# Attention scores from split factors, rope's shifts on ScalarE, softmax one step behind, and two small changes, in a two-layer decoder trunk

## The chip, the core and the metric

The kernel runs on one core of a Trainium2 chip. The core has engines that run side by side, each in the order of its own queue: TensorE (PE in the profile; its weight loads are PEld), VectorE (DVE), ScalarE (ACT), GpSimd (POOL), and SyncE (SP), which issues the transfers. The metric is the time of one execution in device microseconds.

## What is computed

The input is 256 tokens of width 2048. Layer 0 is a gated short convolution and a squared-ReLU MLP; layer 1 is latent attention and another such MLP. After each of the four sublayers `x = LN(ALPHA * x + f(x))`. All is float32.

```
ckv  = h @ w_dkv                                  # 512 latents and 64 rope channels
c    = rms_norm(ckv[..., :512]);  k_pe = rope(ckv[..., 512:])
kv   = c @ w_ukv                                  # 16 heads: k_nope 128, v 128
q    = rms_norm(x @ w_dq) @ w_uq                  # 16 heads: q_nope 128, q_pe 64 (rope)
s    = (q_nope @ k_nope.T + q_pe @ k_pe.T) * 192 ** -0.5      # causal mask
o    = softmax(s) @ v;  out = o @ w_o
mlp  = square(relu(x @ w1)) @ w2                  # 2048 -> 8192 -> 2048
```

## The kernel before

**Split products.** A value is cut into a part `hi`, stored in the type fp32r (ScalarE writes it by a copy), and the rest `lo` (VectorE subtracts). A product is then three fp32r products, hi by hi, lo by hi and hi by lo, and PE makes each in one record. A few small products are made from plain f32 instead; each of these is two records on PE. Weights come in units of 512 KB into six buffers (`raws`), are split into a ring of eight (`whl`), and are taken in the order of the list `stream` (`take`).

**Order of the work.** Most of the program is written in the order in which it is wanted, and a scheduler at build time places each engine's instructions by that order and by when their inputs should be ready. Inside the MLPs the order is made by the kernel's own planner (`Work.arrange`): it has a list of operations with costs and due times, and simulates when each could run. At the start of the program `WARM` f32 products of ones are made while the first data are on their way; then the first four weight columns are multiplied as rows of x arrive (`ps_g`).

**Norms.** Before a sublayer's result is added, `Norm.prepare` scales a row block of `xres` by ALPHA and subtracts a mean taken from the first block (`mu0p`, one f32 product with a square of ones). For the norm after the first MLP (index 1) these sixteen operations stand in the planner's list. `to_wide` then turns the MLP's result by transposes and adds it.

**Latents.** Nine products of 258 columns (`ps_w`, the first three `ps_g`) give four blocks of the keys' latent, one of rope channels (given twice, in both halves of the rows) and four of the queries' latent. `latent` weights them, splits them into `chl` and `qhl`, and sums their squares. `rms` turns a sum of squares into a factor per token, by products of one column (`rstat`) and a root; `rkp` spreads it over the rows, giving `rk`. The keys' latents are split unscaled; `rk` and `rc` come in when keys and values leave PSUM.

**Attention.** `project(g)` makes keys, queries, values and rope queries of four heads, in twelve pieces, and `attention(g - 1)` for the group before runs between them, also in twelve. A head's `attend` has three pieces: the scores `S` of two query blocks (128 queries against 128 keys, 128 against 256) with the softmax; the transposes of the probabilities (`tp`); the product with the values (`po`). The scores are four plain f32 products. After the last group the output projection begins (`out_first`, `ps_wo`).

**Rope.** VectorE multiplies by the cosines, then multiplies each quarter of 32 rows by the sines while it writes it into the neighbouring quarter, then adds.

In the kernel's printed form, a helper records most operations on the engines, so nearly all rows of the profile have its line, L71, and are told apart by their tiles. The tiles `kqva` are the arrays of keys, queries, values and probabilities; `lat` are the latents; `nu` is a step of the norm.

Of the kernel before, what the change touches and what calls it, by code (L numbers as in the profile page):

```python
# [44 lines left out]
GROUP = 3  # L45
WARM = 6
WO_G = 3
# [6 lines left out]
def trunk(ctx: ExitStack, tc: tile.TileContext, opening, xT, vecs, w_in, w_out, w_kv, w_q, w_uk, w_uv,  # L54
# [321 lines left out]
    class Norm:  # L376
# [3 lines left out]
        def __init__(self, idx, scale):  # L380
            self.idx, self.scale = idx, scale
            self.S = act.tile([P, T], F32, tag="S", name=f"S{idx}")
            self.Q = act.tile([P, T], F32, tag="Q", name=f"Q{idx}")
            self.mu0 = act.tile([P, T], F32, tag="mu0", name=f"mu0{idx}")
            self.ws = None

        def prepare(self, m):
# [383 lines left out]
    def mlp(idx, ln, after, blocks, fast):  # L771
# [111 lines left out]
        for k in todo:  # L883
# [181 lines left out]
        def put(n, t, ps):  # L1065
            vector.tensor_tensor(block(n, t), block(n, t), ps, ALU.add)
# [31 lines left out]
    with tc.tile_pool(name="att", bufs=1) as ap:  # L1098
        lat = array("c", F32R, "lat", 2 * NK, 2 * T)
        chl, qhl = ([lat[:, k, :] for k in range(o, o + NK)] for o in (0, NK))  # L1100
        kpe = ap.tile([P, 2, T], F32, name="kpe")
        nc.gpsimd.memset(kpe, 0.0)
        rc = ap.tile([P, 2], F32, name="rc")
# [5 lines left out]

        def rope(dst, src, rows):  # L1110

            a = tmp.tile([P, T], F32, tag="sq", name="ropea")
            b = tmp.tile([P, T], F32, tag="nu", name="ropeb")
            vector.tensor_tensor(a[rows], src[rows], cos_t[rows], ALU.mult)
            for s in range(rows.start, rows.stop, 32):
                d = s ^ 32
                vector.tensor_tensor(b[d:d + 32], src[s:s + 32], sin_t[s:s + 32], ALU.mult)
            vector.tensor_tensor(dst[rows], a[rows], b[rows], ALU.add)

        def latent(ps, m, dst, gcol, sqs):  # L1120
            f = tmp.tile([P, T], F32, tag="fh", name="lat", bufs=3)
            ln.weighted(ps, f)
            g = vec[:, gcol + m:gcol + m + 1]
            scalar.activation(dst[m][:, :T], f, AF.Copy, scale=g)
            vector.scalar_tensor_tensor(dst[m][:, T:], f, g, dst[m][:, :T].bitcast(F32),
                                           ALU.mult, ALU.subtract)
            if m == 0:
                scalar.activation(sqs, f, AF.Square)
            else:
                sq = tmp.tile([P, T], F32, tag="sq", name="sq")  # L1130
                scalar.activation(sq, f, AF.Square)
                vector.tensor_tensor(sqs, sqs, sq, ALU.add)

        def rms(out, sqs):
# [6 lines left out]
            rsqrt(out, ve)  # L1141

        csq = act.tile([P, T], F32, tag="S", name="csq")
        qsq = act.tile([P, T], F32, tag="Q", name="qsq")
# [39 lines left out]
        oT = [ot[:, k, :] for k in range(H)]  # L1184
        kq, vp = (array(a, F32, f"kqv{a}", NC * W) for a in ("a1", "a2"))
        k2, q2, v2 = ([r[:, o:o + 1024].rearrange("p (j t) -> p j t", j=J) for o in (b, b + 1024)]
                      for r, b, J in ((kq, 0, 4), (kq, 2048, 4), (vp, 0, 2)))
        p2 = [vp[:, o:o + 512].rearrange("p (j t) -> p j t", j=2) for o in (2048, 2560)]
        pr2 = [vp[:, o:o + 3 * P] for o in (3072, 3456)]

        with tc.tile_pool(name="att2", bufs=2) as a2, \
                tc.tile_pool(name="paux", bufs=1, space=PS) as paux:
            def project(g, box):

                k4, q4, p4, v4 = (t[g % 2] for t in (k2, q2, p2, v2))
                box.update(k=k4, q=q4, p=p4, v=v4)
# [12 lines left out]
                if g == 0:  # L1209
                    query_scale()  # L1210
                for _ in range(2):
                    ln.normal(next(todo))
                w = take()
# [6 lines left out]
                w = take(1)  # L1220
                for j in range(2):
                    ps = psum("ps_p")
                    mm(ps, w, 4 * j, qhl, NK)
                    rope(p4[:, j, :], ps[:, :T], slice(0, P))
                    yield

            def attend(h, box):

                j = h % 4
                qn, kn = box["q"][:, j, :], box["k"][:, j, :]  # L1230
                qp, kp = box["p"][:, j // 2, :], kpe[:, h % 2, :]
# [6 lines left out]
                pr = pr2[h % 2]  # L1238
                mx = small.tile([P, 2], F32, tag="mx", name="mx")
# [25 lines left out]
            def attention(g, box):  # L1265
                gens = [attend(4 * g + j, box) for j in range(4)]
                for step in range(6):
                    for j in range(3, -1, -1):
                        if 0 <= step - j < 3:
                            next(gens[j])  # L1270
                            yield

# [165 lines left out]
```

## Time and profile before

| | us |
|---|---|
| median of three runs | 2000.35 (1997.7 to 2000.36) |
| the profiled execution | 2000.64 |
| its span, first to last instruction | 1998.8 |
| PE busy in it | 1981.9 (99%) |
| VectorE busy | 1763.3 (88%) |
| ScalarE busy | 1392.6 (70%) |

The mean granted TensorE clock is 0.998. Three kinds of rows are used below. A stage's row gives the stretch, its length, and the busy us of PE, PEld, DVE, ACT and POOL with their counts, then the granted clock, the share of the DMA engines and GB/s. A row of the chain of work that ended last gives start, length, and what ran; a count stands for pieces that follow each other. A group's row gives engine, operation, output and inputs, shape, count, then busy us and the mean ns of one, then the idle time ahead of it with what ended it. Records of products overlap: one lasts longer than the distance to the next.

### The profile page before, as it was taken

Reading aid. Unit: us, or ns where it says so; the run is one execution under the profiler, and the core shown is the slowest. Engines: PE = TensorE matmul, PEld = TensorE weight load, DVE = VectorE, ACT = ScalarE, POOL = GpSimd, SP = SyncE. Lnnn points to the kernel's source line nnn. Section 1 sums busy time; section 2 is a strip of 40 time slices with the busy share of each in tenths; the row PEclk is TensorE's granted clock in tenths of the full one; section 3 lists DMA queues with packets and bytes.
Section 4 is the critical chain, followed back from the end, with each engine's and each line's share of the span. In section 5 each row is a group of like instructions: output and inputs, shape, how many; then the busy total and the mean of one; then the engine's idle time right before and its main releaser. Section 6 shows DMA issues by size and latency. Waiting matters only on the chain.

```text
span 1998.8 us, 29668 instructions
## 1 busy us (share of the span) xinstructions
PE 1981.9 (99%) x11048; PEld 1733.6 (87%) x11048; DVE 1763.3 (88%) x2646; ACT 1392.6 (70%) x2070; POOL 2.3 (0%) x21
## 2 busy tenths in 40 slices
PE   9999999999999999999999999999999999999997
PEld 8888888988888888888889998898888888888886
DVE  7667667699999999999988888878999999999997
ACT  6444445577887888878856655557788888878871
POOL 0000000000000000000000000000000000000000
PEclk9999999999999999999999999999999999999999
DMA  9655555455666666666664543654666666666673
GB/s 337 230 189 187 189 190 188 155 164 185 208 200 208 203 200 201 203 208 205 214 218 156 165 126 115 209 161 156 196 204 198 204 202 208 205 204 203 199 240 119
DMA packets 107857, 387.39 MB, mean 194 GB/s; under 512 B 11968, under 2 KB 12736, under 8 KB 107712
## 3 DMA queue, kind: packets, MB, share of 16 engines
q1 hardware_dynamic: 107568, 385.36, 60.5%
q8 instruction: 86, 1.41, 0.3%
q14 instruction: 59, 0.48, 0.1%
q10 hardware_dynamic: 144, 0.13, 0.0%
HBM read 383.35 MB, written 2.10 MB: 193 GB/s over the span
## 4 chain that ended last, share of the span: by engine, by line
PE 85%; DVE 8%; ACT 3%; issue 2%; DMA 0%; DVEq 0%; ACTq 0%
PE ps_m L71 25%; PE sum L71 21%; PE ps_u L71 20%; PE ps_d L71 4%; PE ps_w L71 4%; PE ps_g L71 4%; DVE lo L71 4%; DVE w L71 2%; ACT hi L71 1%; PE ps_v L71 1%; PE ps_q L71 1%; PE S L71 1%; PE ps_k L71 1%; PE ps_wo L71 1%; ACT sums L71 1%
## 5 line engine op out<-in xcount | busy, mean ns | idle before, releaser
L71 DVE TENSOR_TENSOR lo<-w,hi 128x1024 fp32r<-128x1024 f32 x536 | 640.0, 1222 | 27.2 <-ACT hi L71 24.3
L71 ACT CAST hi<-w 128x1024 fp32r<-128x1024 f32 x536 | 530.8, 1055 | 141.7 <-DVE w L71 131.5
L71 ACT CAST hi<-raw 128x1024 fp32r<-128x1024 f32 x278 | 289.8, 1051 | 248.8 <-PE ps_u L71 154.9
L71 PE MATMUL ps_m<-xhl,hi 128*128 128x512 f32 x1792 | 446.3, 391 | 1.3 <-ACT hi L71 1.3
L71 DVE TENSOR_TENSOR lo<-raw,hi 128x1024 fp32r<-128x1024 f32 x278 | 334.0, 1222 | 112.3 <-ACT hi L71 39.6
L71 PEld LDWEIGHTS ps_m<-xhl,hi 128*128 128x128 f32 x1792 | 328.9, 188 | 65.6 <-ACT hi L71 1.9
L71 PE MATMUL sum<-hi,hc 128*128 128x512 f32 x736 | 277.9, 391 | 0.5 <-ACT sum L71 0.5
L71 PEld LDWEIGHTS ps_m<-xhl,lo 128*128 128x128 f32 x1792 | 244.3, 190 | 18.0 <-DVE lo L71 0.7
L71 PE MATMUL sum<-lo,hc 128*128 128x512 f32 x656 | 256.5, 391 | 0.0
L71 PE MATMUL ps_m<-xhl,lo 128*128 128x256 f32 x1792 | 250.0, 282 | 0.0
L71 PE MATMUL sum<-hi,ha 128*128 128x512 f32 x640 | 246.4, 389 | 0.0
L71 DVE TENSOR_TENSOR w<-w,w 128x512 f32<-128x512 f32 x312 | 214.5, 687 | 0.7
L71 PE MATMUL ps_u<-xhl_a,hi 128*128 128x512 f32 x704 | 168.1, 391 | 0.0
L71 PEld LDWEIGHTS sum<-hi,hc 128*128 128x128 f32 x736 | 138.6, 188 | 27.2 <-ACT sum L71 1.3
L71 PEld LDWEIGHTS ps_u<-xhl_a,hi 128*128 128x128 f32 x704 | 129.4, 188 | 25.1
L71 PEld LDWEIGHTS sum<-hi,ha 128*128 128x128 f32 x640 | 120.2, 188 | 25.9
L71 PEld LDWEIGHTS sum<-lo,hc 128*128 128x128 f32 x656 | 123.6, 188 | 21.5
L71 ACT COPY sums<-sum 128x512 f32<-128x512 f32 x194 | 109.7, 597 | 13.2 <-PE sum L71 12.6
L71 ACT COPY sum<-sums 128x512 f32<-128x512 f32 x174 | 104.3, 611 | 0.8
L71 ACT ACTIVATE sf<-sf 128x512 f32<-128x512 f32 x120 | 76.7, 639 | 26.9 <-DVE sf L71 25.8
L71 PE MATMUL ps_w<-xd,hi 128*128 128x258 f32 x512 | 94.3, 284 | 0.5 <-DVE xres L71 0.5
L71 PEld LDWEIGHTS ps_u<-xhl_a,lo 128*128 128x128 f32 x704 | 90.3, 191 | 3.4
(197 smaller groups left out, 2756.4 us busy)
## 6 DMA issues: line engine op xcount, KB each, us to landing
w<-in_w_dram SPq DMA_DIRECT2D x224, 512.0 KB, 3.9
w<-in_w2f_dram SPq DMA_DIRECT2D x208, 512.0 KB, 4.6
raw<-in_w_in_dram SPq DMA_DIRECT2D x88, 512.0 KB, 4.4
raw<-in_w_dram SPq DMA_DIRECT2D x64, 512.0 KB, 4.4
raw<-in_w_out_dram SPq DMA_DIRECT2D x32, 512.0 KB, 3.9
raw<-in_w_o_dram SPq DMA_DIRECT2D x32, 512.0 KB, 3.8
raw<-in_w2f_dram SPq DMA_DIRECT2D x16, 512.0 KB, 4.5
row<-in_opening_dram SPq DMA_DIRECT2D x15, 384.0 KB, 4.8
```

The costliest lines, as they stand in the source:

```text
L71: ins = op(*args, **named)
```

## The change

- `WARM` goes from 6 to 10.
- Norm 1 has no `prepare` any more. `means` takes the mean of the first block of `xres` as a column of two f32 products with one column of ones, scaled by -ALPHA. `put` adds it to the down products' sums, and `scaled` multiplies `xres` by ALPHA as it adds the turned result.
- The keys' latents are kept in f32 (`keep`), multiplied by `rk` after all latents, and split then. `rms` for them comes after the second product of the queries' latent, not the first. Keys and values leave PSUM unscaled.
- Keys and queries are split as they leave PSUM, into rings of six and five blocks. The scores are five split products a block: three for the 128 plain channels, two for rope. For rope, `kpe` is split into two tiles, and `pos` has a head's hi part in one half of its rows and its lo part in the other.
- `rope` shifts the quarters by ScalarE copies and multiplies all rows at once; the rope queries are made before the values, and their weights stand earlier in `stream`.
- The probabilities have three buffers instead of two, and a piece of `attend` ends after the exponentials. The step that divides by the sum runs one step later, and the loop has seven steps.

```diff
-WARM = 6
+WARM = 10
...
-        stream += halves(w_uk[g]) + halves(w_qn[g]) + halves(w_uv[g]) + halves(w_qp[g])
+        stream += halves(w_uk[g]) + halves(w_qn[g]) + halves(w_qp[g]) + halves(w_uv[g])
...
+        def means(self):
+            ps = psum("mu0c")
+            for t in range(2):
+                tensor.matmul(ps[:, t:t + 1], xres[:, 0, t * P:(t + 1) * P], ones[:, 0:1], start=True, stop=True)
+            self.off = small.tile([P, 2], F32, tag="off", name="off", bufs=1)
+            vector.tensor_scalar(self.off, ps[:, 0:2], -self.scale, None, ALU.mult)
...
+    def scaled(ps, m):
+        d = xres[:, m, :]
+        vector.scalar_tensor_tensor(d, d, ALPHA, ps, ALU.mult, ALU.add)
...
-        if after is not None:
-            after.prepare(0)
...
-        if after is not None:
-            for k in range(1, NC):
-                add("V", 256, lambda k=k: after.prepare(k), normals.get(k))
...
+                vector.scalar_tensor_tensor(block(n, t), ps, after.off[:, t:t + 1], block(n, t), ALU.add, ALU.add)
+        if after is not None:
+            after.means()
...
-                summed(ln, [ps[:, j * T:(j + 1) * T] for j in range(2)], add, 4 * n + 2 * c)
+                summed(ln, [ps[:, j * T:(j + 1) * T] for j in range(2)], scaled, 4 * n + 2 * c)
...
-            vector.tensor_tensor(a[rows], src[rows], cos_t[rows], ALU.mult)
-            for s in range(rows.start, rows.stop, 32):
-                d = s ^ 32
-                vector.tensor_tensor(b[d:d + 32], src[s:s + 32], sin_t[s:s + 32], ALU.mult)
-            vector.tensor_tensor(dst[rows], a[rows], b[rows], ALU.add)
+            for s in range(0, P, 32):
+                scalar.copy(b[s ^ 32:(s ^ 32) + 32], src[s:s + 32])
+            r = tmp.tile([P, T], F32, tag="fh", name=name, bufs=3)
+            vector.tensor_tensor(a, src, cos_t, ALU.mult)
+            vector.tensor_tensor(b, b, sin_t, ALU.mult)
+            vector.tensor_tensor(r, a, b, ALU.add)
+            return r
...
+            if dst is keep:
+                scalar.activation(keep[:, m, :], f, AF.Copy, scale=g)
...
-            latent(next(pss), m, chl, C_KG, csq)
+            latent(next(pss), m, keep, C_KG, csq)
...
-        for j in range(2):
-            rope(kpe[:, j, :], f, slice(64 * j, 64 * j + 64))
+        f = rope(f, "fper")
+        scalar.copy(kpe[:, 0, :], f)
+        vector.tensor_tensor(kpe[:, 1, :], f, kpe[:, 0, :].bitcast(F32), ALU.subtract)
...
-            if m == 0:
+            if m == 1:
                 rms(rc, csq)
...
+        for m in range(NK):
+            vector.tensor_tensor(keep[:, m, :], keep[:, m, :], rk, ALU.mult)
+            put_split(chl[m], keep[:, m, :])
...
-                    vector.tensor_tensor(k4[:, j, :], ps[:, :T], rk, ALU.mult)
+                    put_split(k4[j], ps[:, :T])
...
-                    scalar.copy(q4[:, j, :], ps[:, :T])
+                    put_split(q4[j], ps[:, :T])
...
+                    r = rope(ps[:, :T], "r")
+                    for i in range(2):
+                        t, mine, other = pos[:, 2 * j + i, :], slice(64 * i, 64 * i + 64), slice(64 - 64 * i, 128 - 64 * i)
+                        scalar.copy(t[mine], r[mine])
+                        vector.tensor_tensor(t[other], r[mine], t[mine].bitcast(F32), ALU.subtract)
...
-                    scalar.activation(v4[:, b, :], ps, AF.Copy, scale=rc[:, b:b + 1])
+                    scalar.copy(v4[:, b, :], ps)
...
+                factors = ((qh, kh), (ql, kh), (qh, kl), (pos[:, j, :], kpe[:, 0, :]), (pos[:, j, :], kpe[:, 1, :]))
...
-                    tensor.matmul(S[:, at:at + n], qn[:, tok], kn[:, :n], start=True, stop=False)
-                    tensor.matmul(S[:, at:at + n], qp[:, tok], kp[:, :n], start=False, stop=True)
+                    for i, (q, k) in enumerate(factors):
+                        tensor.matmul(S[:, at:at + n], q[:, tok], k[:, :n], start=i == 0, stop=i == len(factors) - 1)
...
+                yield
                 vector.reciprocal(su, su)
...
-                for step in range(6):
+                for step in range(7):
                     for j in range(3, -1, -1):
-                        if 0 <= step - j < 3:
+                        if 0 <= step - j < 4:
                             next(gens[j])
-                            yield
+                            if step - j != 1:
+                                yield
```

More of the change, by code (lines that the diff above doesn't have):

```diff
@@ L1065, in put @@
         def put(n, t, ps):
-            vector.tensor_tensor(block(n, t), block(n, t), ps, ALU.add)
+            if after is None:
+                vector.tensor_tensor(block(n, t), block(n, t), ps, ALU.add)
+            else:
+                vector.scalar_tensor_tensor(block(n, t), ps, after.off[:, t:t + 1], block(n, t), ALU.add, ALU.add)
+        if after is not None:
+            after.means()
         h = [(one[:, k // 2, k % 2 * T:(k % 2 + 1) * T], two[:, k // 2, k % 2 * T:(k % 2 + 1) * T]) for k in range(QC)]
@@ L1108, in trunk, with rope @@
         sync.dma_start(mask_t, mask)
-        def rope(dst, src, rows):
+        def rope(src, name):
             a = tmp.tile([P, T], F32, tag="sq", name="ropea")
             b = tmp.tile([P, T], F32, tag="nu", name="ropeb")
-            vector.tensor_tensor(a[rows], src[rows], cos_t[rows], ALU.mult)
-            for s in range(rows.start, rows.stop, 32):
-                d = s ^ 32
-                vector.tensor_tensor(b[d:d + 32], src[s:s + 32], sin_t[s:s + 32], ALU.mult)
-            vector.tensor_tensor(dst[rows], a[rows], b[rows], ALU.add)
+            for s in range(0, P, 32):
[5 more added lines that the diff above has]
+            return r
         def latent(ps, m, dst, gcol, sqs):
@@ L1123, in latent @@
             g = vec[:, gcol + m:gcol + m + 1]
-            scalar.activation(dst[m][:, :T], f, AF.Copy, scale=g)
-            vector.scalar_tensor_tensor(dst[m][:, T:], f, g, dst[m][:, :T].bitcast(F32),
-                                           ALU.mult, ALU.subtract)
+            if dst is keep:
+                scalar.activation(keep[:, m, :], f, AF.Copy, scale=g)
+            else:
+                scalar.activation(dst[m][:, :T], f, AF.Copy, scale=g)
+                vector.scalar_tensor_tensor(dst[m][:, T:], f, g, dst[m][:, :T].bitcast(F32),
+                                               ALU.mult, ALU.subtract)
             if m == 0:
@@ L1141, in rms @@
             rsqrt(out, ve)
+        kq, vp = array("a1", F32R, "kq", 11, 2 * T), array("a2", F32, "vp", 3840)
+        v2 = [vp[:, o:o + 1024].rearrange("p (j t) -> p j t", j=2) for o in (0, 1024)]
+        pr3 = [vp[:, o:o + 3 * P] for o in (2048, 2432, 2816)]
+        keep = vp[:, 1024:2048].rearrange("p (j t) -> p j t", j=4)
         csq = act.tile([P, T], F32, tag="S", name="csq")
@@ L1184, in trunk @@
         oT = [ot[:, k, :] for k in range(H)]
[L1185 to L1189, printed above, removed]
+        pos = ap.tile([P, 4, T], F32R, name="pos")
         with tc.tile_pool(name="att2", bufs=2) as a2, \
@@ L1193, in project @@
             def project(g, box):
-                k4, q4, p4, v4 = (t[g % 2] for t in (k2, q2, p2, v2))
-                box.update(k=k4, q=q4, p=p4, v=v4)
+                k4 = [kq[:, (4 * g + j) % 6, :] for j in range(4)]
+                q4 = [kq[:, 6 + (4 * g + j) % 5, :] for j in range(4)]
+                v4 = v2[g % 2]
+                box.update(k=k4, q=q4, v=v4)
                 w = take()
@@ L1212, in project @@
                     ln.normal(next(todo))
+                w = take(1)
+                for j in range(2):
+                    ps = psum("ps_p")
+                    mm(ps, w, 4 * j, qhl, NK)
+                    r = rope(ps[:, :T], "r")
[4 more added lines that the diff above has]
+                    yield
                 w = take()
@@ L1217, in project @@
                         dot(ps, wide_rows(w[k // 2], k % 2), held(chl[k], b), k == 0, k == NK - 1)
-                    scalar.activation(v4[:, b, :], ps, AF.Copy, scale=rc[:, b:b + 1])
-                    yield
[L1220 to L1224, printed above, removed]
+                    scalar.copy(v4[:, b, :], ps)
                     yield
@@ L1229, in attend @@
                 j = h % 4
-                qn, kn = box["q"][:, j, :], box["k"][:, j, :]
-                qp, kp = box["p"][:, j // 2, :], kpe[:, h % 2, :]
+                (qh, ql), (kh, kl) = ((v[:, :T], v[:, T:]) for v in (box["q"][j], box["k"][j]))
+                factors = ((qh, kh), (ql, kh), (qh, kl), (pos[:, j, :], kpe[:, 0, :]), (pos[:, j, :], kpe[:, 1, :]))
                 S = paux.tile([P, 512], F32, tag="S", name=f"S_{h}", bufs=2)
@@ L1419 @@
         "cosT": np.tile(cos, (4, 1)),
-        "sinT": np.tile(np.concatenate([sin, -sin]), (2, 1)),
+        "sinT": np.tile(np.concatenate([-sin, sin]), (2, 1)),
         "mask": np.concatenate([tri, np.zeros((P, P), np.float32), tri], axis=1),
```

9 lines of the change are left out of this document (4 added, 5 removed).

## The prediction

> **What bounds the kernel now.** I read the page first, then its stages (busy time of each engine in stretches), then PE's waits, then the chain of work that ended last.
>
> ```profile
> PE 1981.9 (99%) x11048; PEld 1733.6 (87%) x11048; DVE 1763.3 (88%) x2646; ACT 1392.6 (70%) x2070; POOL 2.3 (0%) x21
> ```
>
> ```profile
> 413.00:513.00 100.00, 99.82 (x500) 84.66 (x499) 96.63 (x150) 79.35 (x120) 0.00 (x0) 1.00 0.55 173
> 1083.00:1100.00 17.00, 17.00 (x144) 17.00 (x144) 16.81 (x36) 11.90 (x23) 0.00 (x0) 1.00 0.55 176
> 1100.00:1120.00 20.00, 20.00 (x148) 19.02 (x147) 19.34 (x45) 15.52 (x29) 0.00 (x0) 1.00 0.67 212
> 1152.00:1182.00 30.00, 30.00 (x210) 27.94 (x209) 23.25 (x57) 16.91 (x38) 0.00 (x0) 1.00 0.41 124
> 1358.00:1458.00 100.00, 99.68 (x499) 84.53 (x498) 91.28 (x134) 78.26 (x118) 0.00 (x0) 1.00 0.54 171
> ```
>
> ```profile
> PE ps_m L71 <- ACT hi L71: 1.3, 3, 0.9
> PE rstat L71 <- DVE csq L71: 0.8, 1, 0.8
> PE S L71 <- DVE kqva L71: 0.4, 1, 0.4
> ```
>
> PE is full everywhere (columns: length, then busy us of PE, PEld, DVE, ACT, POOL). So only two things move the end: less streaming on PE, or fewer of PE's few waits. A wait that the change adds on PE counts in full. VectorE is full too between 1083 and 1120, where the latents and the first group's keys are made, and has a quarter free in a later attention group (23.25 of 30); ScalarE has much free there (16.91 of 30).
>
> Whole stretches of PE, from the chain (start, length, products):
>
> ```profile
> 5.22 24.43 PE ps_g L71 x128
> 29.65 128.03 PE ps_u L71 x736
> 412.66 10.92 PE sum L71 x48
> 972.37 3.26 PE ps_m L71 x16
> 1357.31 10.92 PE sum L71 x48
> 1916.11 3.27 PE ps_m L71 x16
> ```
>
> ```profile
> 1081.68 0.43 DVE csq L71
> ...
> 1082.15 0.60 PE rstat L71 x4
> 1082.76 11.64 PE ps_w L71 x96
> 1094.40 0.22 PE rkp L71 x2
> 1094.62 5.76 PE ps_w L71 x48
> 1100.38 5.75 PE ps_k L71 x48
> ...
> 1123.23 0.34 DVE kqva L71
> 1123.58 0.14 issue
> 1123.71 2.41 PE S L71 x12
> ...
> 1128.28 1.31 PE S L71 x8
> ```
>
> The profiled execution took 2000.64 us: a span of 1998.8 and 1.8 around it. The median of the three runs is 2000.35, 0.3 below, so I give my sum against the profiled one and take it off the median. A difference of 0.2% (4 us) is about what a measurement of this kernel can tell from no change.
>
> **Scores in five products.** Each f32 product of before runs as two records, so a head's scores are eight records in 1.31 us (the piece at 1128.28). After, there are five split products of 128 columns and five of 256. A split product of 256 columns takes 5.75/48 = 0.120 us (ps_k at 1100.38). A split product of 128 columns does not occur in this trace. What stands nearest:
>
> ```profile
> 1063.35 0.53 PEld L71 LDWEIGHTS stat<-col,S 128*128 128x128 f32 x4
> 1063.80 0.53 PEld L71 LDWEIGHTS stat<-col,Q 128*128 128x128 f32 x4
> ```
>
> ```profile
> L71 PEld LDWEIGHTS ps_k<-lat,hi 128*128 128x128 f32 x128 | 20.1, 191 | 0.2
> L71 PEld LDWEIGHTS stat<-col,S 128*128 128x128 f32 x12 | 1.6, 191 | 0.0
> ```
>
> The statistics stream one column, yet four records take 1063.80 - 1063.35 = 0.45 us, 0.1125 each: that is the pace of weight loads alone. The load in front of a split product lasts as long as that one (191 ns both), so I take the load as the bound and 0.113 us for 128 columns. A head then costs 5 x 0.113 + 5 x 0.120 = 1.165 us, 0.145 less than 1.31; 16 heads: **-2.3 us**. The ends: if the load hid fully, the columns alone would give half of 0.120, 0.060 us, a head 0.90 and the sum -6.6; if 128 split columns ran no faster than a whole f32 product of two records (2 x 0.1125 = 0.225 us, once for each of five), a head would cost 1.725 and the sum be +6.6. The load row is the nearest because it has the same weights and fewer columns.
>
> **Ten warm-up products.**
>
> ```profile
> L71 PE MATMUL warm<-ones 128*128 128x128 f32 x12 | 2.9, 434 | 1.0 <-DVE col L71 1.0
> ```
>
> ```profile
> 1.05 2.93 PE L71 MATMUL warm<-ones 128*128 128x128 f32 x12 [1.05 <-DVE col L71]
> 5.22 1.19 PE L71 MATMUL ps_g<-xhl_a,hifirst 128*128 128x512 f32 x2 [1.25 <-ACT hifirst L71]
> ```
>
> Six warm-ups are twelve records, (2.93 - 0.43)/11 = 0.227 us apart, twice the 0.1125 of the same loads later: PE is slow here. It is still slow when the real work begins: 64 pairs of 512 and 256 columns take 24.43 us at the opening, while 368 pairs of the next stage take 128.03, so 64 should take 22.27. The opening loses 2.16 us. Four more warm-ups are eight records, 1.8 us: the last would start at 1.05 + 19 x 0.227 = 5.36 and stream until about 5.5, so the first real product moves from 5.22 to about 5.5, 0.3 later. If PE is fast from there on, 2.16 - 0.3 = 1.9 is won; I take **-1.6**, as its first products may still be slow. Ends: +0.3 (nothing gets faster) and -1.9. What is late next is not the data: the next stage is PE for 128.03 us on end, so the gain is kept. By the Trainium skill (TensorE: Matmul & The Clock Gate, What's actually happening) the clock opens after a busy window of about 3.4 us that runs free of the kernel; 1.05 to 3.8 is shorter than that and 1.05 to 5.5 longer, and by that rule the gain would differ from run to run, about 0.5 to 1.9 us, an estimate. No row here shows the windows.
>
> **The means' column.** For the first MLP's norm, one f32 product of 256 columns (two records, 0.43 us by the scores' 256-column share: (1.31 - 4 x 0.1125)/2) leaves the stage's start, and two of one column (four records, 4 x 0.1125 = 0.45) come before the first down product: **0**. There, a full bank could hold them back by one evacuation (0.37 and 0.42 us, rows below): I add **+0.1**, ends 0 and 0.8. Fifteen subtractions leave VectorE; the addition of the mean rides on an addition that is made anyway. The second MLP shows what these subtractions cost PE: without them, VectorE has 91.28 us of work in 100 instead of 96.63, and PE is as full (99.68 against 99.82). From the first group to the last chunk the first MLP takes 972.37 - 412.66 = 559.71 us, the second 1916.11 - 1357.31 = 558.80. With the subtractions gone the planner gets the same list for both, so up to 0.9 us can come back; the loss is a late `hi` (0.9 in PE's waits) that hangs on a weight's landing, so I take **-0.5**, ends 0 and -0.9.
>
> **The latents and the wait they bring.** `rms` moves behind the next product, so PE no longer waits for `csq` in front of `rstat`: **-0.9** (0.8 in PE's waits, 1.0 in the load's). But the keys' side is now scaled by `rk` before it is split, so the first `ps_k`, which in this trace needed only latents that had long been ready, now needs `rms`, `rkp`, `rk`, four multiplications and four splits.
>
> ```profile
> 1084.21 0.15 DVE L71 TENSOR_SCALAR rve<-rstat 128x2 f32<-128x2 f32 x1
> ...
> 1090.64 0.16 DVE L71 SCALAR_TENSOR_TENSOR rc<-ra,rt 128x2 f32<-128x2 f32 x1
> ...
> 1105.43 1.43 DVE L71 TENSOR_TENSOR kqva<-ps_k,rk 128x256 f32<-128x256 f32 x4
> ```
>
> ```profile
> L71 DVE TENSOR_TENSOR oT<-po,oT 128x256 fp32r<-128x256 f32 x16 | 6.7, 420 | 2.7 <-ACT oT L71 2.6
> L71 ACT CAST oT<-po 128x256 fp32r<-128x256 f32 x16 | 5.9, 370 | 9.8 <-PE po L71 9.8
> L71 DVE TENSOR_TENSOR ropeb<-ps_p,sin_t 32x256 f32<-32x256 f32 x32 | 13.5, 420 | 0.5
> ```
>
> From `rve` to `rc` VectorE took 6.4 us, mostly in other work queued between. With `rms` one product (5.8 us) later, `rc` comes between 1090 (five short steps with nothing between) and 1095, `rk` 1 us after it, and the eight VectorE operations of 0.36 (1.43/4) another 2.9 us. So the last split is ready between about 1094 and 1099 if they go first, against a need at about 1099.5 (1100.38 less 0.9), and later if other work goes first, which it did to the four `kqva<-ps_k,rk` of before: they started at 1105.43, when the last latent was through. In favour: VectorE loses four of eight operations of the keys' rope and the four early splits there, eight of 0.36 to 0.42, about 3 us, just ahead of this point. Behind the waiting `ps_k` stands all of PE. I take **+1.0**, ends 0 and 6 (the second is a rival).
>
> **Projections.** Each group adds to VectorE four splits of q and takes two of twelve rope operations (a shift of 32 partitions cost as much as a full one, 0.42): +2 x 0.36; to ScalarE four copies of k and twelve for rope: 16 x 0.37 = 5.9 us. In a group of 30 us that makes about 24 and 23: hidden, if nothing stands in the way; in the first group the rope's price is what PE waited for at 1123.71, where scores stood 0.5 us (0.34 + 0.14 in the chain). With `w_qp` taken before `w_uv`, two value products (5.5 us of PE) lie over that: **-0.5**. The reordered loads are the same transfers on one queue. What waits behind ScalarE's shifts are `hi` casts, made well ahead. **Softmax one step behind** takes small waits of the transposes on the exponentials; none is in PE's waits above, so **-0.2**, ends 0 and -1.
>
> Sum: -2.3 - 1.6 + 0.1 - 0.5 - 0.9 + 1.0 - 0.5 - 0.2 = -4.9. From 2000.64 that is 1995.7; from the median, 1995.4.
>
> **Rivals.** (1) The keys wait. If VectorE keeps its order and scales the latents only when the last one is through, then, with 3 us less ahead of it, it starts at about 1102.4 instead of 1105.43, and PE gets its last key latent at 1105.3 instead of 1099.5: +5.8 in place of +1.0, **2000.2**. For it: VectorE is full (16.81 of 17) and those operations are the youngest. Against: its order is chosen by readiness, and `rc` was squeezed in.
> (2) Slower: 128 split columns gain nothing over whole f32 products of 128. Then scores cost +6.6 instead of -2.3: **2004.3**. It decides as soon as a 128-column split product takes over 0.23 us, and it grows with the five products. Against: every split product here of 256 or 512 columns streams at one pace (0.120; 22.27/64 - 0.120 = 0.228), and the load does not know the columns. For: none here has fewer than 256.
> (3) Loads overlap more than the statistics show. Halfway between the two faster ends, at (0.060 + 0.1125)/2 = 0.086 us for 128 columns, a head costs 1.03 and the scores' term is -4.5, 2.2 further down: **1993.2**. For it: the statistics' records are halves of f32 products, whose loads may not overlap like those of split ones; against it stands their equal length. The Trainium skill (TensorE: Matmul & The Clock Gate, Back-to-back issue gap) gives about 81 ns for a sustained 128-column pair of load and product; by that the time would be 1992.8, an estimate, and the 0.1125 us of the statistics' rows speaks against it.
> (4) The warm-ups don't do what they are for: PE stays slow as long after 5.5 as it did after 5.22. Then +0.3 instead of -1.6: **1997.3**.
>
> **How the numbers follow.** Forecast 0.48, keys wait 0.18, slow short products 0.10, faster loads 0.12, warm-ups idle 0.08, none of these 0.04. The forecast's own range, from the ends of its terms without the rivals', is about 1993.5 to 1998. The range 1991.8 to 2000.6 takes in the first, third and fourth rival and leaves out the second and what is in none. Over 0.2% faster means below 1996.35: most of the forecast and all of rival 3, with a rest, 0.60; slower than 2004.35 is half of rival 2 and a tail of rival 1, 0.12; between, 0.28.
>
> **What would show it.** Records of a 128-column score product 0.113 apart and 1.15 to 1.2 us for a head; the opening's 128 products in about 22.5 us, their first at 5.5; no wait of `rstat` for `csq`; the first `ps_k` with a gap of a microsecond at most before it; no gap before the first scores; both MLPs equally long from first group to last chunk. I am wrong if `ps_k` waits several microseconds for VectorE, if short score products are 0.2 apart, or if ScalarE's shifts show up as PE's waits in every group.

## The result: 0.15% slower, and the profile after

The changed kernel takes 2002.8 us in the median of 22 runs (2002.0 to 2003.4); the kernel before took 1999.7 in the same rounds (1997.7 to 2001.8). The ratio is 1.0015 (95% interval 1.0009 to 1.002). I had forecast 1995.4 and a range up to 2000.6. The profiled execution took 2002.36 us, its span 2000.5.

The page of the changed kernel, busy times by engine:

```profile
PE 1984.6 (99%) x11090; PEld 1733.2 (87%) x11090; DVE 1760.9 (88%) x2638; ACT 1417.1 (71%) x2142; POOL 1.7 (0%) x20
```

PE is busy 2.7 us longer than before, though the scores should have taken 2.3 us from it. The chain of work that ended last, of the changed kernel (start, length, what ran):

```profile
5.65 22.42 PE ps_g L71 x128
28.07 128.03 PE ps_u L71 x736
...
443.72 4.82 PE sum L71 x21
...
495.69 4.82 PE sum L71 x21
...
996.72 21.92 PE ps_d L71 x96
...
1209.93 1.15 PE S L71 x10
...
1237.05 72.38 PE ps_u L71 x416
...
1356.98 21.78 PE sum L71 x96
```

and of the kernel before, two pieces of the same loop of the first MLP:

```profile
518.50 4.79 PE sum L71 x21
...
601.28 4.79 PE sum L71 x21
```

The opening is what I forecast (22.42 us, the next stage at 28.07 and not 29.65). But an MLP's loop takes longer: five turns lie between 443.72 and 495.69, 10.394 us each, and eight between 518.50 and 601.28 before, 10.348 each. Of the 51 turns from one such row to the next in each MLP, 47 and 48 take 46 to 48 ns longer, 2.2 us together. In the second MLP one turn that had been longer than the others became 0.3 shorter, which leaves 2.0. Worked out from the first product of each stage in both traces, in us:

| from ... to | before | changed |
|---|---|---|
| start, first ps_u | 29.49 | 27.91 |
| first MLP's products of sums, to the first ps_d | 584.68 | 586.10 |
| first latent ps_w, to ps_u of the output projection | 179.43 | 179.37 |
| second MLP's products of sums, to the first ps_d | 586.99 | 588.99 |
| everything else | 618.26 | 618.12 |

So two things need a cause. Both MLPs are slower, the second by 2.0 us although it makes the same operations; and latents with attention gained nothing. PE's waits in the changed kernel, then two of ScalarE's (the waiting tile, what ended the wait, us in all, times, longest), and the latter of the kernel before:

```profile
PEld po L71 <- DVE oT L71: 4.8, 8, 0.9
PE po L71 <- DVE oT L71: 2.3, 5, 0.5
...
ACT vp L71 <- DVE mx L71: 19.3, 16, 2.0
```

```profile
ACT kqva L71 <- DVE mx L71: 6.1, 7, 1.6
```

The wait of `rstat` on `csq` and that ahead of the first scores are gone. In their place the values' products `po` wait in every group until VectorE has evacuated the head before into `oT`: the distance from one product to the next is too long there in seven places, by 0.24 to 0.65 us, 3.6 together.

### The profile page after: what moved, and what is told of

It is laid out like the page before. It is cut to its first block, busy times and chain, and to the rows that moved or that the text cites. A ratio compares the mean times of both kernels' runs of the same rounds, so it can differ in the third digit from the quotient of the medians.

```text
span 2000.5 us, 29806 instructions
## 1 busy us (share of the span) xinstructions
PE 1984.6 (99%) x11090; PEld 1733.2 (87%) x11090; DVE 1760.9 (88%) x2638; ACT 1417.1 (71%) x2142; POOL 1.7 (0%) x20
## 4 chain that ended last, share of the span: by engine, by line
PE 91%; DVE 4%; ACT 3%; issue 1%; DVEq 0%; ACTq 0%
PE ps_m L71 30%; PE sum L71 26%; PE ps_u L71 20%; PE ps_d L71 4%; PE ps_g L71 4%; PE ps_w L71 4%; DVE lo L71 1%; ACT hi L71 1%; PE ps_wo L71 1%; ACT vp L71 1%; ACT ropeb L71 1%; DVE mx L71 0%; PE turned L71 0%; DVE vp L71 0%; DVE nu L71 0%
```

## Experiments

Each ran in five rounds beside the kernel before, whose median was 1999.8 to 2000.2 us.

### The loss in the MLPs is an address

One difference between the two builds reaches both MLPs: the tile `off`, 8 bytes padded to 32, stands among the small tiles, and everything allocated behind it lies 32 bytes further on. `t4` is among these. It holds a combination of a weight's blocks, split into hi and lo, and is the sixth of the seven that PE streams in each turn (the text below calls it activations; the kernel writes weights into it). The tile's instructions in the second MLP, of the kernel before and of the changed one (duration in ns: min/median/max):

```profile
L71 PE MATMUL sum<-t,hc x88: 389/389/389, 1445.2 to 1891.0; 128*128 128x512 f32 x88
```

```profile
L71 PE MATMUL sum<-t,hc x88: 393/396/399, 1445.1 to 1892.6; 128*128 128x512 f32 x88
L71 PE MATMUL sum<-t,ha x44: 397/397/397, 1445.6 to 1892.8; 128*128 128x512 f32 x44
```

**off twice.** In the changed kernel:

```
- self.off = small.tile([P, 2], F32, tag="off", name="off", bufs=1)
+ self.off = small.tile([P, 2], F32, tag="off", name="off", bufs=2)
```

> The changed kernel, with one thing different: the small tile off is given two buffers instead of one, so what is allocated behind it lies 64 bytes further on than in the kernel before, not 32. Theory (address): in the changed kernel the tile t4 (the activations that the sum products stream) starts at an odd multiple of 32 bytes, and each 512-column product that streams it takes about 9 ns longer, 46.7 ns in every 10.35-us period of both MLPs, some 84 periods. At a multiple of 64 the loss goes: 2002.8 - 3.9 = about 1998.9, the distance of sum products on t4 back from 236 to 227 ns, the period back to 10.347 us. Rival (the means or the order of the MLPs): the loss comes from the work that the change moved there, and an address does nothing: 2002.8, period 10.393.

Measured 2004.65 (ratio to before 1.0023, 1.0013 to 1.0032): 1.9 more, not 3.9 less. My first form of the theory, multiples of 64, fell. The rival fell too, since two buffers instead of one moved the time.

**Unused tile alone.** In the kernel before, in `mlp`:

```
+ if after is not None:
+     pad = small.tile([P, 2], F32, tag="pad", name="pad", bufs=1)
+     vector.memset(pad, 0.0)
```

> The kernel before, plus one unused tile of 8 bytes a partition among the small tiles, set to zero once in the first MLP; what is allocated behind it moves by 32 bytes. Theory (address): t4 loses 46.7 ns in each of some 84 periods, so about +3.9 us on the before of the same rounds, 2003.6, and the period goes from 10.347 to 10.393 us, in both MLPs. Rival (means or order): one small operation of VectorE costs nothing, 1999.7.

Measured 2003.69 (1.0017, 1.0008 to 1.0026), 3.6 more than before. Eight unused bytes cost about what was forecast, and the second MLP takes 588.99 us, to the hundredth what the changed kernel takes.

**off in a constant tile.** In the changed kernel, with nothing moved:

```
+ self.off = col[:, 2:4]
```

> The changed kernel with off kept in two spare columns of a constant tile, so that nothing behind it moves: every large tile starts where it did before (all of them at multiples of 128 bytes). A shift of 64 bytes was slower still than one of 32, so an odd multiple of 32 is not the point; the theory now is that any start off a multiple of 128 costs. Theory (address): the periods return to 10.347 us, 3.9 us come back, 1998.9; since ten warm-ups alone gave 1998.1, what is left of the change is worth -0.2 to +0.8. Rival (the order of the MLPs or the change's code, not addresses): 2002.8 as the changed kernel.

Measured 1998.72 (0.9995, 0.9986 to 1.0004), 4.1 less than the changed kernel; the second MLP takes 586.95. This is the whole loss. Against the kernel before of its rounds (1999.77) the rest of the change is worth 1.05 us, with an interval that takes in no gain at all.

**t4 alone.** In the kernel before:

```
- fast.tile([P, 2, BW], F32R, tag="t4", name="t4", bufs=1)
+ fast.tile([P, 2 * BW + 8], F32R, tag="t4", name="t4", bufs=1)[:, 8:]...
```

> The kernel before, with 32 unused bytes at the start of the tile t4 alone, the last in its pool: t4's data begin 32 bytes on, and nothing else moves. Theory (the address of what PE streams): the whole loss of the unused tile among the small ones, +3.5 to +3.9 us on before, 2003.5, in the same products (those on t4 and the six or so after them), the period 10.393. Rival (the tiles sf, which ScalarE and VectorE work on, disturb PE from their new place): +0, 1999.8, period 10.347.

Measured 2003.9 (1.0018, 1.001 to 1.0027), the second MLP 588.96. Moving t4 alone costs all of it, so it is t4's own place and not that of the tiles on which ScalarE and VectorE work.

**off four times** (`bufs=4` in the changed kernel, a shift of 128 bytes):

> The changed kernel with four buffers for off: everything behind it moves by 128 bytes. Theory (a start off a multiple of 128 bytes costs): no loss, 1998.7 as with off in a constant tile, t4's products at 227 ns and the period at 10.347 to 10.366 us. Rival (any move from the kernel before's addresses costs, growing with the distance: 32 bytes 3.9 us, 64 bytes 5.9): 2005 or more.

Measured 2001.93 (1.0009, 1.0 to 1.0017): 3.2 more than in a constant tile. Multiples of 128 are not the point either, and the loss doesn't grow with the distance.

**t4 moved by 256 bytes** (as t4 alone, with 64 columns in place of 8) and **t4 first** (t4 in a pool of its own, opened ahead of that of `sf`):

> The kernel before, with 256 unused bytes at the start of t4 alone. In the kernel before, all large tiles that PE reads in the MLPs (weights hi and lo, activations hc and ha, t4) start 128 bytes behind a multiple of 256, and 640 behind one of 1024; here t4 keeps the first and loses the second. Theory A (the place within 256 bytes must agree): no loss, 1999.9. Theory B (the place within 1024 bytes or more must agree): +3 to +6, 2003 to 2006. Rival C (any move costs): the same as B here.

> The kernel before, with t4 allocated ahead of the two sf tiles instead of behind them: t4 lies 8192 bytes lower, the sf tiles 4096 bytes higher, so every place within 4096 bytes agrees as before. Theories A and B: no loss, 1999.9, period 10.347 us. Rival C (any move from the kernel before's place costs): +3 to +6.

Measured 2000.31 (0.9999, 0.999 to 1.0008) and 2000.59 (1.0, 0.9992 to 1.0009). Theory A fits and B and C fell: t4 can move by 256 bytes or by 8192 without loss, and loses at 32, 64 and 128. Whether its place within 256 bytes has to agree with that of the other tiles, as A puts it, or counts by itself, these runs don't tell. The tile's rows with t4 moved by 128 bytes (off four times), and by 256:

```profile
L71 PE MATMUL sum<-t,hc x88: 386/392/396, 1445.1 to 1892.2; 128*128 128x512 f32 x88
L71 PE MATMUL sum<-t,ha x44: 397/398/399, 1445.5 to 1892.4; 128*128 128x512 f32 x44
```

```profile
L71 PE MATMUL sum<-t,hc x88: 389/389/389, 1445.5 to 1891.3; 128*128 128x512 f32 x88
```

### The opening

**Warm-ups alone** (`WARM = 10` in the kernel before):

> The kernel before with ten warm-up products instead of six and nothing else. Theory (the warm-ups do in every run what they did in the profile): -1.6 us, 1998.1, and a narrower spread than before's 1997.7 to 2001.8, since the opening no longer depends on when the clock opens. Rival (the clock's phase differs from run to run, and before's runs catch it early in part): the median gains less, 0.3 to 1.0 us, and the best run of before is not beaten. Second rival (idle): +0.3.

Measured 1998.12 (0.999, 0.9981 to 0.9999), with runs between 1997.55 and 1999.27. The gain in the median is 2.0, more than in the profile's opening, and the spread is narrower. This run keeps the old norm, and yet its first MLP takes 584.19 us against 584.68 before; that matters for a term of the prediction (below). The chain's opening with six warm-ups in two other profiles, unused tile alone and t4 alone, and with ten in the run with off in a constant tile:

```profile
5.18 22.67 PE ps_g L71 x128
27.85 128.05 PE ps_u L71 x736
```

```profile
5.01 24.18 PE ps_g L71 x128
29.20 128.05 PE ps_u L71 x736
```

```profile
5.59 22.44 PE ps_g L71 x128
28.04 128.03 PE ps_u L71 x736
```

With six, the same opening is fast in one profile (27.85) and slow in the other (29.20), and the latest of the six-warm-up profiles ends it at 29.9. With ten the next stage began between 27.8 and 28.6 in every profile. So in a single execution ten warm-ups can lose 0.7 us or win 2.1, and what they do is to take away the slow openings. The fast one is of the run whose tiles lie 32 bytes further on, but the place alone doesn't seem to decide it: that run's executions spread from 2001.59, which is the profiled one, to 2004.62. The rule in the Trainium skill (TensorE: Matmul & The Clock Gate, What's actually happening) of a window that runs free of the kernel agrees, in that the gain differs from run to run. The granted clock reads 1.00 over the first 12 us of every profile, with six warm-ups and with ten, so no row here shows the window itself.

### Latents and attention

**Old attention** (the kernel before with ten warm-ups and the means' column, off twice):

> The kernel before with ten warm-up products and the means' column, and off in two buffers (a shift of 64 bytes); latents, projections, scores and softmax as before. It isolates what the attention part of the change is worth, by comparison with the run that has the whole change and off in two buffers. Theory (attention's gain of 2.3 us of streaming is eaten by new waits of PE): this run takes the same time as that one within 0.8 us, about 1999, its stretch from first latent product to output projection 194.0 us as in both. Rival (attention gains its forecast 3 us, and only the addresses lost it): this run is 2.5 to 3 us slower than that one, about 2001.

Measured 2004.71, against 2004.65 with the new attention and the same shift of 64 bytes. The attention part is worth nothing, as the theory said; the time of both (about 1999 was forecast) is higher because 64 bytes cost too. Nor did an address hide a gain: from the first latent `ps_w` to the output projection it is 179.22 and 179.36 us in these two, and 179.43 and 179.44 in the kernel before and in the run with off in a constant tile, where nothing moved.

**po in halves of its bank**, on the run with off in a constant tile:

```
- po = paux.tile([P, 512], F32, tag="tb", name="po")
+ po = pot[:, h % 2 * T:(h % 2 + 1) * T]      # pot: one tile for all heads
```

> The run with off in a constant tile, and the values' products po of consecutive heads in the two halves of their one PSUM bank instead of all in its first half: po need not wait until the head before has been evacuated into oT. Theory (the attention's gain is lost in po's wait for oT): PE's and its loads' waits on oT, 7.1 us in the changed kernel of which some 3.6 are gaps between products, go; 2.5 to 3.6 us less than the run with off in a constant tile, about 1995.5, and the stretch of projections and attention 3 us shorter. Rival (po waits because everything behind ScalarE's shifts is late; the next late thing takes its place): within 0.7 us of that run.

Measured 1998.69; PE's waits of `po` on `oT` stood as they were (5.1 us on the loads and 2.3 on the products, against 5.1 and 2.2). The build, it seems, orders accesses by the whole bank. So this run says nothing about the theory.

**po in the ring:**

```
+ po = psum("po")
+ tp = paux.tile([P, 512], F32, tag="ta", name="tp", bufs=2)
```

> The run with off in a constant tile, and the values' products po in the ring of four banks that the projections use, the transposes tp in two banks. (Halves of one bank had changed no wait: the build treats a bank as one, so po still waited.) Theory (po waits for its one bank): the seven gaps of 0.3 to 0.65 us ahead of po, 3.6 us together, go, and the run takes 1995.5 to 1996.5, 2 to 3 us less than with one bank. Rival (VectorE is late as a whole; the ring's bank four back, or pt, is next): no more than 0.7 us less.

Measured 1998.05 (0.9991, 0.9982 to 1.0). In its trace the stretch from the latents to the output projection is 0.8 us shorter (178.63). Its waits of PE:

```profile
PEld po L71 <- DVE kq L71: 1.6, 3, 0.7
...
PEld ps_q L71 <- DVE kq L71: 1.2, 3, 0.5
```

The wait on `oT` shrank, and the splits `kq` that use the same ring came next. The rival (no more than 0.7) held: 0.67 less in the median.

**Shifts on VectorE** and **softmax in the same step**, on the run with off in a constant tile:

```
- scalar.copy(b[s ^ 32:(s ^ 32) + 32], src[s:s + 32])
+ vector.tensor_tensor(b[d:d + 32], src[s:s + 32], sin_t[s:s + 32], ALU.mult)
```

> The run with off in a constant tile, and the rope's shifts on VectorE as before (four multiplications of 32 rows by the sines, written into the neighbouring quarter, in place of four copies on ScalarE and one multiplication). Theory (ScalarE's shifts hold up the evacuations behind them): 1.5 to 3 us less, about 1996.5, waits on oT mostly gone. Rival (VectorE, which gets three operations of 0.42 us more for each shift set, is then late instead): same or up to 1.5 us more.

```
- for step in range(7):          # and the yield ahead of the reciprocal
+ for step in range(6):
```

> The run with off in a constant tile, and the softmax finished in the same step as before (the division by the sums not one step later, six steps and not seven a group). Theory (softmax one step behind, not the shifts, puts the next head's exponentials in front of the evacuation of po): 1 to 3 us less, about 1997, and the waits of po on oT mostly gone. Rival (the later step is harmless or helps the transposes): same, or 0.5 to 1.5 us more with new waits of tp on the probabilities.

Measured 2006.85 (1.0033, 1.0021 to 1.0044) and 2002.27 (1.0013, 1.0004 to 1.0021), 8.1 and 3.6 more. Both theories fell, and both costs are far above what the rivals allowed: with the rest of the change in place, each of the two parts is needed. PE's waits of the one and the other:

```profile
PE po L71 <- DVE oT L71: 4.7, 4, 1.8
...
PE ps_k L71 <- ACT lat L71: 2.4, 1, 2.4
PE tp L71 <- DVE vp L71: 2.0, 1, 2.0
```

```profile
PE tp L71 <- DVE vp L71: 4.3, 4, 1.3
...
PE po L71 <- DVE oT L71: 1.7, 3, 0.6
```

**No lo parts** and **no shifts in the last two groups**, on the run with off in a constant tile:

```
- put_split(k4[j], ps[:, :T])
+ put_split(k4[j], ps[:, :T]) if g < 2 else scalar.copy(k4[j][:, :T], ps[:, :T])     # no lo parts; the same for q4
...
- r = rope(ps[:, :T], "r")
+ r = rope(ps[:, :T], "r", g < 2)     # no shifts: without the copies where this is false
```

> The run with off in a constant tile, leaving out VectorE's subtraction in the splits of keys and queries in the last two groups (the lo parts of earlier heads stay there): 16 operations of 0.42 us less on VectorE. Theory (the evacuations of po are late because VectorE is loaded by the new splits): the four gaps ahead of po in those two groups, 1.9 us together, go or halve, 1.0 to 1.9 us less than that run. Rival (it is ScalarE's queue): within 0.4 us of it.

> The run with off in a constant tile, leaving out ScalarE's shift copies of the query rope in the last two groups (the sines are multiplied with unshifted rows): 16 copies of 32 rows less on ScalarE. Theory (the evacuations wait behind ScalarE's shifts): the same four gaps go or halve, 1.0 to 1.9 us less than that run. Rival (VectorE's queue): within 0.4 us of it.

Measured 2001.75 and 1998.85. Without the shifts nothing changed (+0.1), and with 16 operations fewer on VectorE the time was 3.0 us longer, which neither theory nor rival had. VectorE in the run with off in a constant tile, and in that without lo parts, at the same head (start, length, operation, in brackets idle time and what ended it):

```profile
1165.64 0.17 DVE L71 RECIPROCAL su<-su 128x2 f32<-128x2 f32 x1 [1.30 <-ACT vp L71]
1165.84 0.29 DVE L71 TENSOR_SCALAR vp<-vp,su 128x128 f32<-128x128 f32 x1
1166.04 0.42 DVE L71 TENSOR_TENSOR kq<-ps_q,kq 128x256 fp32r<-128x256 f32 x1
1166.38 0.41 DVE L71 TENSOR_TENSOR oT<-po,oT 128x256 fp32r<-128x256 f32 x1
```

```profile
1165.21 0.17 DVE L71 RECIPROCAL su<-su 128x2 f32<-128x2 f32 x1 [1.30 <-ACT vp L71]
1165.41 0.55 DVE L71 TENSOR_SCALAR vp<-vp,su 128x128 f32<-128x128 f32 x2
1166.42 1.22 DVE L71 TENSOR_TENSOR lo<-raw,hi 128x1024 fp32r<-128x1024 f32 x1 [0.45 <-ACT hi L71]
1167.56 0.42 DVE L71 TENSOR_TENSOR oT<-po,oT 128x256 fp32r<-128x256 f32 x1
```

The evacuation is short (0.41) but stands in line. In both, VectorE first idles 1.30 us for another head's exponentials; with two small operations gone the scheduler put a weight's `lo` ahead of `oT`, 1.22 us and its wait, and PE's gap ahead of `po` grew from 0.29 to 1.6 us, here and in the next group. That is the place in the queue at work. Since load and order changed at once, this run can't tell what less load alone would do. ScalarE's queue in the run with off in a constant tile shows the other half:

```profile
1164.43 0.49 ACT L71 ACTIVATE vp<-vp,mx,sc 128x128 f32<-128x128 f32 x1 [1.88 <-DVE mx L71]
...
1165.76 0.37 ACT L71 CAST oT<-po 128x256 fp32r<-128x256 f32 x1
```

ScalarE stands idle for 1.88 us at an exponential that waits for VectorE's maximum, with the cast of `oT` behind it.

**Reciprocal behind**, **oT on VectorE**, and the latter with **po in the ring**, on the run with off in a constant tile:

```
+ tc.add_manual_dep(...)      # su's reciprocal behind the last oT on VectorE
+ tc.add_manual_dep(...)      # each exponential behind the last cast of oT on ScalarE (the first run only)
- scalar.copy(oT[h][:, :T], po[:, :T])
+ vector.tensor_copy(oT[h][:, :T], po[:, :T])      # the second and third run only
```

> The run with off in a constant tile, and on VectorE the softmax's reciprocal of a head held, by an order edge, behind the last evacuation into oT that is written before it; no operation is added or left out. In the queues this puts oT ahead of su in each group's first evacuation, but leaves it behind a weight's hi and lo in the second. Theory (order: an evacuation waits behind whatever the build put ahead of it): the gaps of 0.29 us ahead of po go to 0.1, those of 0.65 stay, 0.3 to 0.6 us less than that run. Rival (load): nothing.

> As the run with the reciprocal behind, and both parts of oT made on VectorE (a copy for hi, then the subtraction), so that ScalarE's exponentials and casts no longer stand ahead of it; VectorE gets 16 operations of about 0.42 us more, and in its queue oT now stands ahead of the weight's lo in the second evacuation too. Theory (order): PE's waits of po on oT drop from 3.6 us of gaps to 1 or less although VectorE has more to do, 1.5 to 2.5 us less than the run with off in a constant tile, about 1996.7. Rival (load: VectorE is late because it has too much): same or up to 2 us more.

> The same as oT on VectorE with the reciprocal behind, and po in the projections' ring of banks. Theory (order and bank together): all gaps ahead of po go, 2.5 to 3.5 us less than the run with off in a constant tile, about 1995.7. Rival (load): no better than the ring alone, 1998.1, or worse.

The first run's edit does more than its text says: it also holds the exponentials on ScalarE behind the cast of `oT`.

Measured 1998.87, 1998.53 (0.9993, 0.9984 to 1.0002) and 1998.06 (0.999, 0.9981 to 0.9999). No theory's time came; all three lie, within the noise, where the rivals put them. With the reciprocal behind, the gaps of 0.29 us went below 0.15 as forecast, but three of the others grew by 0.05 to 0.07, and the stretch stayed at 179.44. With oT on VectorE PE's wait of `po` on `oT` fell to 0.2 us, but the trace now puts 2.3 us of it down to `su`, and the stretch is 0.7 shorter (178.77), not 1.5 to 2.5. PE's waits of the last of the three:

```profile
PEld tp L71 <- DVE vp L71: 1.2, 3, 0.7
PEld po L71 <- DVE kq L71: 1.1, 2, 0.6
PEld ps_q L71 <- DVE kq L71: 1.1, 3, 0.5
```

So an edge in the order moves a wait, and one cure uncovers the next: the traces show which wait ends last each time, but not what would have to change for the group as a whole to be faster. Too much work on VectorE is not the plain answer, since 16 operations more there cost no time. Nothing tried got back more than 0.8 of the 3.6 us. The best versions (po in the ring, oT on VectorE with it, and ten warm-ups alone, 1998.05 to 1998.12) are 1.9 to 2.1 us faster than the kernel before of their rounds and cannot be told apart; for po in the ring the interval reaches 1.0. The ten warm-ups are thus all of the change that is seen to pay.

## Why the prediction was wrong, step by step

The miss is 7.4 us: 4.1 from t4's address (2002.8 against 1998.72), 3.3 from the rest, of which the attention is 2.9. The 1998.72 would have lain inside my range, but by luck: not for the reasons that made up the forecast.

- **Means' column, 0 + 0.1: the step that failed first.** I priced its operations and not its tile. A profile of before shows no address; the diff shows a new tile, and I passed over it. It cost 4.1, more than any term of the sum. The operations themselves did what I had said: the stretch ahead of the first MLP's sums is 0.2 shorter in every profile with the column (382.6 for 382.8), that from the first down product to the first latent `ps_w` 0.1 longer (60.9 for 60.8).
- **Projections, "hidden": the second failure.** I set sums of busy time (23 and 24 in 30 us) against the length of a group. They came out (below), and still `po` waits, 3.6 us of gaps in seven places. In the queues above, the evacuation that `po` needs stands in line behind operations that wait for the other engine; a sum of busy time does not see that. What the other terms won, about 3.4 by the rows (2.6 at the scores, 0.8 and 0.5 for the two waits, less 0.5 for the keys), went there. My sign of a fault, ScalarE's shifts as PE's waits in every group, half came true: the waits are in every group, but not due to the shifts.

```profile
1100.00:1120.00 20.00, 19.70 (x142) 18.50 (x142) 18.52 (x42) 15.89 (x35) 0.00 (x0) 1.00 0.54 173
1152.00:1182.00 30.00, 29.39 (x218) 27.62 (x217) 25.29 (x64) 23.54 (x57) 0.00 (x0) 1.00 0.39 123
```

- **Scores, -2.3: right.** A head took 1.15 us (the piece at 1209.93) against my 1.165. Most of its products of 128 columns begin 0.110 to 0.115 us apart, the pace that the statistics' loads had (0.1125); neither rival 2 nor rival 3 happened.
- **Ten warm-ups, -1.6: right in the profile** (28.07 against 29.65), 2.0 in the median of the run that has them alone. Rival 4 fell.
- **rms later, -0.9, and scores after w_qp, -0.5: right**, both waits are gone. The keys' wait, +1.0, was 0.2 at `ps_k`, with 0.5 at the first `ps_q` behind the keys' splits; rival 1 fell. It was not far off: with the shifts on VectorE `ps_k` waited 2.4 us.
- **Softmax a step behind, -0.2: mis-sized.** I read its worth off the old attention's waits, where the transposes hardly wait. In the new one it is worth 3.6: without it PE's transposes `tp` wait four times for the probabilities, 4.3 us.
- **First MLP as long as the second, -0.5: not shown.** In ten profiles with the column and t4 in place the first MLP takes 584.03 to 584.74 us (median 584.07), in four with the subtractions and t4 in place 584.19 to 584.94 (584.74). But all ten have ten warm-ups, and of the four only one has, which takes 584.19: as short as the run with off in a constant tile (584.22), with the subtractions still there. By the prediction's own measure, first group to last chunk, its two MLPs take 559.21 and 558.77 us. So about half of the 0.9 that I put down to the subtractions was gone with ten warm-ups alone; what the column adds is open.

The attention's terms made -2.9 together, and the run with the old attention shows 0.

## What to carry to other kernels

When a change adds or removes a tile, however small, compare the address lists of the two builds before anything else, and keep a few bytes of scratch in a tile that exists. An engine with a quarter of its time free can still hold up PE: look at what its queue has ahead of the one operation that PE needs. Where two engines hand a head back and forth, look at which of them stands idle with that operation behind it. And run each small part of a change alone: here one of them gave all of the gain that was seen.

## What the runs showed of the hardware

With t4 moved by 32 bytes, each of the three 512-column products that stream it stands about 231 to 236 ns from the next one, not 226.7, and the five after them are slow too. The distances of these five (230, 236, 228, 232, 231, then 227 on) are within 3 ns those that the kernel before shows after each run of 256-column products (233, 236, 228, 232, 231). At 64 bytes at least nine products behind t4's are slow. Shifts of 32, 64 and 128 bytes cost 2.0, 3.2 and 1.7 us in the second MLP; 256 and -8192 nothing. The Trainium skill (SBUF — State Buffer, Operand start alignment) asks only for a multiple of the element size and says that this is about legality, not speed; these runs add a speed. Why the place within 256 bytes matters, and whether it counts by itself or must agree with the stream before or with the loaded operand, stays open: no run moved all of them together.
